# Hybrid decoder trunk: products with v of two pairs of heads in one run

## The chip, the cores and the metric

The kernel runs on one core of a Trainium2 chip. The time is device microseconds of that core, as the median of several executions; one further execution is taken with the hardware profiler, and all durations below come from it. The engines are named as in the profile: PE is TensorE's matmuls, PEld its weight loads, DVE VectorE, ACT ScalarE, POOL GpSimd, SP SyncE.

## What is computed

A trunk of two layers over 256 tokens of width 1024. Each layer normalises its input, projects it, and feeds two mixers: a recurrence (RG-LRU, four blocks of 128 channels here) and an attention with 8 query heads of 64 and 2 key/value heads. Each mixer's output is multiplied by a SiLU gate, and both go through one output projection onto the residual. Cut to what matters for the change:

```python
o_c = einsum('bghqk,bgkd->bghqd', p_c, vc)      # compressed blocks
o_s = einsum('bghqk,bgqkd->bghqd', p_s, vg)     # selected blocks
o_w = einsum('bghqk,bgkd->bghqd', p_w, vwb)     # sliding window
y_b = (gb[..., 0:1] * o_c + gb[..., 1:2] * o_s + gb[..., 2:3] * o_w)
y_b = y_b * silu(nsa_gate)
y = concatenate([y_a, y_b], axis=-1)
return x + y @ w_out
```

## The kernel before

**Tiling.** Activations are held with channels on the 128 partitions and the 256 tokens along the free dimension. A weight is split into a high and a low part (`wh`, `wl`), and so are the activations that it multiplies, so that every large product is three matmuls, made by `mm3` (lines 173 to 175). Two heads, one for each key/value head, share the 128 partitions of a tile; such a pair is called i, and there are four.

**Steps.** A layer is a list of 33 steps, each with one chunk of weights that is loaded, split and multiplied. Steps 0 to 11 of the list `plan` are the twelve chunks of `wf` (three kinds: x and g for the recurrence, n for the attention's gate); 12 to 15 are the first four chunks of the output projection (`out_proj`, half 0, on the recurrence's part of y). Four more chunks of `out_proj` follow (half 1, on the attention's part). The dictionary `SL` (line 53) says ahead of which step each piece of the attention and of the recurrence is written in the program: `att_scores`, `att_coef`, `att_turn`, `att_out`, `rg_gates` and so on. The framework that builds the kernel takes this order as a priority. It sets the order on each engine when the kernel is built, by its own reckoning of when inputs and buffers are ready, and puts in all waits; at run time each engine then works strictly in that order.

**The attention's pieces around the change.** For pair i and token half t:

- `att_scores` and `att_coef` (lines 567 to 607) make scores, exponentials and weights. The last ACT instruction is line 605, which scales the probabilities `pr`.
- `att_turn` (line 609) transposes them on TensorE (line 618) into a `pp` bank, and ACT copies them into the tile `pt` of pair i (`copy`, line 83). `pt` has two buffers, so two pairs can be held at a time.
- `att_out(i)` (line 623) multiplies them with v. The result takes 256 columns of the one PSUM bank of tag `m`. Ten matmuls of 64 output columns each are made, in twos that fill the lower and the upper 64 partitions: per branch two of 256 tokens (line 628) and two of 128 (line 631), then two with the compressed branch's probabilities `pct` (line 634). In the profile each of them has two records, since these operands are plain f32.
- DVE then multiplies the bank with the gate `sgn` into a tile of tag `tmp` (line 636), and `y_split` (line 559) makes the high part on ACT (line 560) and the low part on DVE (line 561), in slot 4 + i of `yy`.

The `m` bank has one buffer. It is used before by the compressed branch (`cmp_scores`, `cmp_pt`) and by each `att_out` in turn, so the next user's matmuls wait until the one before has been read. Before the change, `att_out` stands ahead of steps 6, 7, 12 and 15. Tiles of tag `tmp2` (`pair`, line 227; 128 x 2 x 256, three buffers) are used by the gates, by `rg_gates`, by `rg_out` and, near the layer's end, by the squares for the next norm.

`out_proj` of half 1 needs all four slots of the attention's part. Its first chunk takes the slots 0 to 2 for both output halves first, and slot 3 last (lines 710 to 717), because pair 3 comes last, ahead of step 15.

Of the kernel before, what the change touches and what calls it, by code (L numbers as in the profile page):

```python
# [15 lines left out]
ALU = mybir.AluOpType  # L16
AX = mybir.AxisListType

P = 128
D = 1024  # L20
S = 256
# [3 lines left out]
HD = 64  # L25
# [13 lines left out]
for _n, _w in (("g", 8), ("cw", 16), ("cb", 4), ("br", 4), ("bi", 4), ("lam", 4)):  # L39
# [12 lines left out]
K = dict(scale="A", ev1="A", hid="A", pct="A")  # L52
SL = dict(qk=(0, 2), order=("x0", "x1", "x2", "x3", "n0", "n1", "g0", "g1", "g2", "g3", "n2", "n3"),
          cmp=(2, 3, 4), att=(1, 3, 3, 4, 6, 7, 10, 11), turn=(2, 4, 5, 6, 8, 10,
          12, 13), cs=(5, 5), cpt=6, aout=(6, 7, 12, 15), gates=(2, 3, 4, 5), tab=6, sqrt=5,
          scan=8, rout=(9, 11))


# [13 lines left out]
def hybrid_trunk_kernel(ctx: ExitStack, tc: tile.TileContext, vx, wc, wt, wv, wf, wo, w1, w2, pe,  # L72
# [6 lines left out]
    V, A, G, T = nc.vector, nc.scalar, nc.gpsimd, nc.tensor  # L79
# [7 lines left out]
    def act(shape, tag, bufs=1, dt=F32):  # L87
        return ap_.tile(shape, dt, name=tag, tag=tag, bufs=bufs)

    def bank(tag, bufs, shape=(P, 512), dt=F32):  # L90
        return ps.tile(list(shape), dt, name=tag, tag=tag, bufs=bufs)
# [20 lines left out]
    for n in range(8):  # L112
        T.matmul(wb.rearrange("p (a s) -> p a s", a=2), wz[:, :P], wz[:, None].to_broadcast([P, 2, S]),
                 start=n == 0, stop=n == 7)
# [57 lines left out]
    def mm3(o, lh, ll, rh, rl, start, stop):  # L172
        T.matmul(o, lh, rh, start=start, stop=False)  # L173
        T.matmul(o, lh, rl, start=False, stop=False)  # L174
        T.matmul(o, ll, rh, start=False, stop=stop)  # L175
# [35 lines left out]
    def h_tiles():  # L211
        return act([P, KT, S], "hh", 1, F32R), act([P, KT, S], "hl", 1, F32R)

    def h_split(l, h, k):
        A.activation(h[0][:, k], x_sb[:, k], AF.Copy, scale=v(l, "g", k))
        V.scalar_tensor_tensor(h[1][:, k], x_sb[:, k], v(l, "g", k), h[0][:, k].bitcast(F32),
                               op0=ALU.mult, op1=ALU.subtract)
# [9 lines left out]
    def pair(dt=F32):  # L227
        return act([P, 2, S], "tmp2", 3, dt)
# [27 lines left out]
    def layer(l, prev):  # L256

        L = Layer()
# [300 lines left out]
        def y_split(k, yt):  # L559
            A.copy(L.yy[:, 0, k], yt)  # L560
            V.tensor_tensor(L.yy[:, 1, k], yt, L.yy[:, 0, k].bitcast(F32), op=ALU.subtract)
# [58 lines left out]
                copy(K["ev1"] if c else "A", L.pts[i][:, :, :, t + c],  # L620
                     pp.rearrange("p (g b s) -> p g b s", g=2, b=2))

        def att_out(i):
            pt = L.pts.pop(i)
            yb = L.yb = bank("m", 1)
            for b in range(2):
                for g in range(2):
                    T.matmul(yb[g * HD:(g + 1) * HD, :S], L.vv[:, 0, b, g * HD:(g + 1) * HD],  # L628
                             pt[:, g, b, 0:2].rearrange("p a s -> p (a s)"), start=(b == 0), stop=False)
                for g in range(2):  # L630
                    T.matmul(yb[g * HD:(g + 1) * HD, P:S], L.vv[:, 1, b, g * HD:(g + 1) * HD],
                             pt[:, g, b, 2], start=False, stop=False)
            for g in range(2):
                T.matmul(yb[g * HD:(g + 1) * HD, :S], L.vcb[:, 2 * i + g], L.pct, start=False, stop=True)
            yt = act([P, S], "tmp", 3)
            V.tensor_tensor(yt, yb[:, :S], L.sgn[:, i], op=ALU.mult)
            y_split(4 + i, yt)


        def rg_x(j):  # L640
# [53 lines left out]
        def out_proj(c, half, n):  # L694
            if half and n == 0 and l + 1 < DEPTH:
                L.nh, L.nsq = h_tiles(), act([P, S], "pct")
            last = half and l + 1 == DEPTH and n == 3
            os_ = bank(*OB[half][n])
            os_ = (os_, bank(*FM)) if last else (os_, os_)

            def region(e):
                return os_[e][:, :S] if last else os_[e][:, e * S:(e + 1) * S]

            def products(e, ks):
                for k in ks:
                    mm3(region(e), c.hi[:, k, e * P:(e + 1) * P], c.lo[:, k, e * P:(e + 1) * P],
                        L.yy[:, 0, 4 * half + k], L.yy[:, 1, 4 * half + k],
                        k == 0 and (last or e == 0), k == 3 and (last or e == 1))

            if half and n == 0:  # L710
                products(0, range(3))
                products(1, range(3))
                ks = [3]
            else:
                ks = range(4)
            for e in range(2):
                products(e, ks)
                m = slice(2 * n, 2 * n + 2)
                if last:
                    m = slice(2 * n + e, 2 * n + e + 1)  # L720
                    V.tensor_tensor(x_sb[:, m], x_sb[:, m], region(e)[:, None], op=ALU.add)
                elif e:
                    V.tensor_tensor(x_sb[:, m], x_sb[:, m], os_[0].rearrange("p (a s) -> p a s", a=2), op=ALU.add)  # L723
                else:
                    continue
                if half and l + 1 == DEPTH:
                    nc.sync.dma_start(out[:, m], x_sb[:, m])
                elif half:
                    sk = pair()
                    A.activation(sk, x_sb[:, m], AF.Square)  # L730
                    for k in (2 * n, 2 * n + 1):
                        h_split(l + 1, L.nh, k)
                    if n == 0:
                        L.sk0 = sk
                    else:
                        V.tensor_tensor(L.sk0, L.sk0, sk, op=ALU.add)
                    if n == 3:
                        V.tensor_tensor(L.nsq, L.sk0[:, 0], L.sk0[:, 1], op=ALU.add)
# [8 lines left out]
        for k in range(KT):  # L747
            b = []
# [22 lines left out]
        def at(n, f, *a, mid=False):  # L771
            plan[n][1 if mid else 0].append(F(f, *a))
# [6 lines left out]
        for q in range(8):  # L779
            i, t = divmod(q, 2)  # L780
# [5 lines left out]
        for q in range(8):  # L786
            at(SL["turn"][q], att_turn, *divmod(q, 2))
        for i in range(4):
            at(SL["aout"][i], att_out, i)
            at(SL["gates"][i], rg_gates, i)  # L790
        at(SL["tab"], next_gains, mid=True)
        at(SL["sqrt"], rg_sqrt, mid=True)
# [10 lines left out]
        for half in range(2):  # L803
            for n in range(4):
                step(Chunk(wo[l, 4 * half + n], 4, 256, dma=True),
                     R(out_proj, half, n), None, *(plan[12 + n] if half == 0 else ([], [next_tables] if n == 1 else [])))
# [3 lines left out]
    for l in range(DEPTH):  # L810
        prev, st_ = layer(l, prev)
        prev0 = prev0 or prev
        steps += st_
# [140 lines left out]
```

## Time and profile before

| | |
|---|---|
| median of 3 runs | 253.13 us (252.58 to 253.38) |
| time of the profiled execution | 252.82 us |
| span in that execution, first to last instruction | 251.0 us |
| PE, share of the span with a matmul in flight | 97% |
| DVE, ACT, POOL | 78%, 66%, 16% |
| matmuls of `att_out`, lines 628, 631, 634: records | 64, 64, 32 |
| their mean durations | 392, 273, 379 ns |
| granted TensorE clock | full through the whole span |

The page gives busy time by engine, then groups of instructions by line and shape. A matmul's duration there includes the time in which it shares the array with its neighbours: two that follow one another start 0.12 us apart although each is shown with 0.28. So for TensorE the starts in the time-ordered view are what counts, and the durations of lines tell little. A name such as `m<-pt,vv` gives the tile that is written and those that are read; `128*64` is the weight tile's shape, `128x256` the moving operand's. A bracket behind a row gives the idle time of the engine ahead of it and the instruction that ended it.

### The profile page before, as it was taken

Reading aid. Unit: us, or ns where it says so; the run is one execution under the profiler, and the core shown is the slowest. Engines: PE = TensorE matmul, PEld = TensorE weight load, DVE = VectorE, ACT = ScalarE, POOL = GpSimd, SP = SyncE. Lnnn points to the kernel's source line nnn. Section 1 sums busy time; section 2 is a strip of 40 time slices with the busy share of each in tenths; the row PEclk is TensorE's granted clock in tenths of the full one; section 3 lists DMA queues with packets and bytes.
Section 4 is the critical chain, followed back from the end, with each engine's and each line's share of the span. In section 5 each row is a group of like instructions: output and inputs, shape, how many; then the busy total and the mean of one; then the engine's idle time right before and its main releaser. Section 6 shows DMA issues by size and latency. Waiting matters only on the chain.

```text
span 251.0 us, 5217 instructions
## 1 busy us (share of the span) xinstructions
PE 243.0 (97%) x1958; PEld 222.2 (88%) x1958; DVE 195.8 (78%) x386; ACT 164.5 (66%) x419; POOL 40.1 (16%) x65
## 2 busy tenths in 40 slices
PE   7999998999999999999999999998999999999994
PEld 3989997977899798999999999996889879989993
DVE  4898798879999997654995569688999998765422
ACT  5966419799999967622873553849999996670000
POOL 0034460001811011000001044100100001010000
PEclk9999999999999999999999999999999999999999
DMA  6987999856699688562569878475249858833022
GB/s 211 371 289 226 318 413 407 265 168 202 195 322 403 184 266 293 174 202 72 167 207 347 312 236 263 159 230 187 93 167 347 317 177 268 271 127 84 3 84 84
DMA packets 17593, 57.17 MB, mean 228 GB/s; under 512 B 2208, under 2 KB 3360, under 8 KB 17056
## 3 DMA queue, kind: packets, MB, share of 16 engines
q1 hardware_dynamic: 12816, 39.86, 46.4%
q0 software_dynamic: 4608, 16.78, 20.9%
q8 instruction: 15, 0.25, 0.4%
q10 hardware_dynamic: 144, 0.20, 0.2%
q14 instruction: 10, 0.08, 0.1%
HBM read 55.78 MB, written 1.05 MB: 226 GB/s over the span
## 4 chain that ended last, share of the span: by engine, by line
PE 59%; DVE 19%; ACT 12%; DMA 4%; issue 2%; POOL 1%; SPq 0%; DVEq 0%; ACTq 0%
PE fm L173 11%; PE fm L175 10%; PE fm L174 10%; DVE wl L168 6%; PE s L174 4%; PE s L175 4%; PE s L173 4%; ACT pr L592 3%; PE m L628 3%; PE pp L618 3%; DMA raw<-in_wt_dram 2%; DMA raw<-in_wf_dram 2%; DVE cx L649 2%; POOL st L179 1%; DVE sm L584 1%
## 5 line engine op out<-in xcount | busy, mean ns | idle before, releaser
L168 DVE TENSOR_TENSOR wl<-raw,wh 128x1024 fp32r<-128x1024 f32 (+4 forms) x67 | 74.4, 1117 | 7.9 <-PE pp L174 3.0
L173 PE MATMUL fm<-hh,wh 128*128 128x256 f32 x192 | 56.9, 296 | 0.2
L174 PE MATMUL fm<-hl,wh 128*128 128x256 f32 x192 | 55.0, 287 | 0.0
L175 PE MATMUL fm<-hh,wl 128*128 128x256 f32 x192 | 54.5, 284 | 0.5 <-DVE wl L168 0.5
L165 ACT CAST wh<-raw 128x768 fp32r<-128x768 f32 (+4 forms) x35 | 30.8, 883 | 28.6 <-DMA raw<-in_wc_dram 7.6
L173 PEld LDWEIGHTS fm<-hh,wh 128*128 128x128 f32 x192 | 36.7, 191 | 2.1 <-issue 1.2
L175 PEld LDWEIGHTS fm<-hh,wl 128*128 128x128 f32 x192 | 36.7, 191 | 1.2 <-DVE wl L168 0.8
L174 PEld LDWEIGHTS fm<-hl,wh 128*128 128x128 f32 x192 | 36.7, 191 | 0.5 <-issue 0.4
L592 ACT ACTIVATE pr<-s,sm 128x128 f32<-128x128 f32 (+1 forms) x64 | 26.0, 417 | 9.4 <-DVE sm L586 6.0
L173 PE MATMUL fm<-yy,wh 128*128 128x256 f32 x96 | 27.4, 285 | 0.0
L175 PE MATMUL fm<-yy,wl 128*128 128x256 f32 x96 | 26.8, 279 | 0.0
L174 PE MATMUL fm<-yy,wh 128*128 128x256 f32 x96 | 26.8, 279 | 0.0
L605 ACT ACTIVATE pr<-pr,sm 128x128 f32<-128x128 f32 (+1 forms) x64 | 23.7, 455 | 1.8 <-DVE sm L598 1.8
L173 PEld LDWEIGHTS fm<-yy,wh 128*128 128x128 f32 x96 | 18.0, 188 | 1.5 <-DVE sm L597 0.8
L156 POOL DMA_DIRECT2D wh<-in_wo_dram x16 | 8.5, 530 | 66.2 <-PE fm L175 29.1
L174 PEld LDWEIGHTS fm<-yy,wh 128*128 128x128 f32 x96 | 18.1, 188 | 0.0
L175 PEld LDWEIGHTS fm<-yy,wl 128*128 128x128 f32 x96 | 18.0, 188 | 0.0
L174 PE MATMUL s<-wl,hh 128*128 128x384 f32 x48 | 16.5, 344 | 0.3 <-DVE wl L168 0.3
L723 DVE TENSOR_TENSOR head<-head,fm 128x512 f32<-128x512 f32 x11 | 7.5, 686 | 11.5 <-PE fm L175 11.5
L156 POOL DMA_DIRECT2D wh<-in_wf_dram x16 | 9.0, 565 | 46.2 <-PE fm L175 24.4
L175 PE MATMUL s<-wh,hl 128*128 128x384 f32 x48 | 16.2, 337 | 0.0
L173 PE MATMUL s<-wh,hh 128*128 128x384 f32 x48 | 15.6, 353 | 0.3 <-ACT wh L165 0.3
(205 smaller groups left out, 615.0 us busy)
## 6 DMA issues: line engine op xcount, KB each, us to landing
raw<-in_wf_dram SPq DMA_DIRECT2D x24, 512.0 KB, 4.5
wh<-in_wf_dram POOLq DMA_DIRECT2D x16, 512.0 KB, 4.8
raw<-in_wo_dram SPq DMA_DIRECT2D x16, 512.0 KB, 5.0
wh<-in_wo_dram POOLq DMA_DIRECT2D x16, 512.0 KB, 4.5
raw<-in_wt_dram SPq DMA_DIRECT2D x15, 384.0 KB, 3.9
yy<-in_w_dram SPq DMA_DIRECT2D x4, 1024.0 KB, 7.4
raw<-in_wc_dram SPq DMA_DIRECT2D x4, 512.0 KB, 5.2
raw<-in_wv_dram SPq DMA_DIRECT2D x4, 420.0 KB, 4.9
```

The source lines that it names most:

```text
L156: G.dma_start(self.wh, self.src)
L165: A.copy(hi[:, c], self.raw[:, c])
L168: V.tensor_tensor(lo[:, c], self.raw[:, c], hi[:, c].bitcast(F32), op=ALU.subtract)
L173: T.matmul(o, lh, rh, start=start, stop=False)
L174: T.matmul(o, lh, rl, start=False, stop=False)
L175: T.matmul(o, ll, rh, start=False, stop=stop)
L592: A.activation(pr[g][:, b], ov[:, b], AF.Exp, bias=sm[:, 0, 2 * g + b:2 * g + b + 1], accum_out=sm[:, 1, 2 * g + b:2 * g + b + 1])
L605: A.activation(pr[g][:, b], pr[g][:, b], AF.Copy, scale=sc_)
L618: T.transpose(pp[:, (2 * g + b) * P:(2 * g + b + 1) * P], pr[g][:, b, c * P:(c + 1) * P], ident)
L628: T.matmul(yb[g * HD:(g + 1) * HD, :S], L.vv[:, 0, b, g * HD:(g + 1) * HD], pt[:, g, b, 0:2].rearrange("p a s -> p (a s)"), start=(b == 0) ...
L649: V.scalar_tensor_tensor(cx[:, j], xp[:, 1 + k:1 + k + S], v(l, "cw", 4 * k + j), cx[:, j], op0=ALU.mult, op1=ALU.add)
L723: V.tensor_tensor(x_sb[:, m], x_sb[:, m], os_[0].rearrange("p (a s) -> p a s", a=2), op=ALU.add)
```

## The change

`att_out` now handles two pairs of heads, u = 0 for pairs 0 and 1, u = 1 for pairs 2 and 3. Their products go to the two halves of one `m` bank in one run of twenty matmuls; only the first matmul of the bank for each 64 partitions has the start flag. Then there is one gate product over 512 columns into a `tmp2` tile, and one `y_split` over two slots. The two calls stand ahead of steps 7 and 15. The first chunk of `out_proj`'s half 1 takes the slots 0 and 1 first and then 2 and 3.

```diff
-          12, 13), cs=(5, 5), cpt=6, aout=(6, 7, 12, 15), gates=(2, 3, 4, 5), tab=6, sqrt=5,
+          12, 13), cs=(5, 5), cpt=6, aout=(7, 15), gates=(2, 3, 4, 5), tab=6, sqrt=5,
...
-        def att_out(i):
-            pt = L.pts.pop(i)
-            yb = L.yb = bank("m", 1)
-            for b in range(2):
+        def att_out(u):
+            yb = bank("m", 1)
+            for h in range(2):
+                i = 2 * u + h
+                pt = L.pts.pop(i)
+                o = yb[:, h * S:(h + 1) * S]
+                for b in range(2):
+                    for g in range(2):
+                        T.matmul(o[g * HD:(g + 1) * HD], L.vv[:, 0, b, g * HD:(g + 1) * HD],
+                                 pt[:, g, b, 0:2].rearrange("p a s -> p (a s)"), start=h == b == 0, stop=False)
+                    for g in range(2):
+                        T.matmul(o[g * HD:(g + 1) * HD, P:], L.vv[:, 1, b, g * HD:(g + 1) * HD],
+                                 pt[:, g, b, 2], start=False, stop=False)
                 for g in range(2):
-                    T.matmul(yb[g * HD:(g + 1) * HD, :S], L.vv[:, 0, b, g * HD:(g + 1) * HD],
-                             pt[:, g, b, 0:2].rearrange("p a s -> p (a s)"), start=(b == 0), stop=False)
-                for g in range(2):
-                    T.matmul(yb[g * HD:(g + 1) * HD, P:S], L.vv[:, 1, b, g * HD:(g + 1) * HD],
-                             pt[:, g, b, 2], start=False, stop=False)
-            for g in range(2):
-                T.matmul(yb[g * HD:(g + 1) * HD, :S], L.vcb[:, 2 * i + g], L.pct, start=False, stop=True)
-            yt = act([P, S], "tmp", 3)
-            V.tensor_tensor(yt, yb[:, :S], L.sgn[:, i], op=ALU.mult)
-            y_split(4 + i, yt)
+                    T.matmul(o[g * HD:(g + 1) * HD], L.vcb[:, 2 * i + g], L.pct, start=False, stop=h == 1)
+            yt = pair()
+            V.tensor_tensor(yt, yb.rearrange("p (a s) -> p a s", a=2), L.sgn[:, 2 * u:2 * u + 2], op=ALU.mult)
+            y_split(slice(4 + 2 * u, 6 + 2 * u), yt)
...
             if half and n == 0:
-                products(0, range(3))
-                products(1, range(3))
-                ks = [3]
+                products(0, range(2))
+                products(1, range(2))
+                ks = [2, 3]
...
         for i in range(4):
-            at(SL["aout"][i], att_out, i)
+            if i < 2:
+                at(SL["aout"][i], att_out, i)
             at(SL["gates"][i], rg_gates, i)
```

## The prediction

> **What bounds the kernel now.** I read the page's first two lines, then a table of busy time by stretch, then the instructions in order of time around the code that changes. In the page, busy time and its share of the span:
>
> ```profile
> span 251.0 us, 5217 instructions
> PE 243.0 (97%) x1958; PEld 222.2 (88%) x1958; DVE 195.8 (78%) x386; ACT 164.5 (66%) x419; POOL 40.1 (16%) x65
> ```
>
> In the table by stretch (length, then busy time of each engine, granted clock, DMA share, GB/s), the stretches that hold the changed code:
>
> ```profile
> 80.00:86.00 6.00, 6.00 (x58) 4.38 (x58) 6.00 (x9) 5.97 (x18) 0.53 (x1) 1.00 0.85 285
> 99.00:116.00 17.00, 17.00 (x153) 15.35 (x152) 9.74 (x15) 7.78 (x19) 1.06 (x2) 1.00 0.59 191
> 200.00:205.00 5.00, 4.88 (x50) 3.16 (x48) 4.97 (x9) 4.97 (x14) 0.53 (x1) 1.00 0.56 170
> 205.00:248.00 43.00, 42.43 (x362) 39.94 (x360) 25.34 (x42) 15.50 (x46) 2.65 (x5) 1.00 0.44 140
> ```
>
> TensorE (PE) has work in every one of them, at full clock; DVE and ACT are full only around the first two products of a layer. So what changes TensorE's own time there changes the end by as much. But "busy" only says that some matmul is in flight. What a matmul costs is the distance from one start to the next. The first run of att_out, in order of time (start, duration, line, tile, count):
>
> ```profile
> 80.53 0.28 PE L175 MATMUL fm<-hh,wl 128*128 128x256 f32 x1
> 80.65 0.28 PE L173 MATMUL fm<-hh,wh 128*128 128x256 f32 x1
> 80.86 0.44 PE L628 MATMUL m<-pt,vv 128*64 128x256 f32 x2
> ...
> 81.12 0.39 PE L628 MATMUL m<-pt,vv 128*64 128x256 f32 x2
> 81.34 0.39 PE L631 MATMUL m<-pt,vv 128*64 128x128 f32 x4
> 81.56 0.39 PE L628 MATMUL m<-pt,vv 128*64 128x256 f32 x2
> ...
> 81.78 0.39 PE L628 MATMUL m<-pt,vv 128*64 128x256 f32 x2
> ...
> 82.21 0.39 PE L634 MATMUL m<-pct,vcb 128*64 128x256 f32 x2
> ...
> 82.42 0.39 PE L634 MATMUL m<-pct,vcb 128*64 128x256 f32 x2
> 82.74 0.66 PE L618 MATMUL pp<-cst,pr 128*128 128x128 f32 x4
> 83.15 0.36 PE L174 MATMUL fm<-hl,wh 128*128 128x256 f32 x1
> ```
>
> And the second run's end:
>
> ```profile
> 85.15 0.60 PE L634 MATMUL m<-pct,vcb 128*64 128x256 f32 x4
> 85.68 0.38 PE L175 MATMUL fm<-hh,wl 128*128 128x256 f32 x1
> 85.90 0.28 PE L173 MATMUL fm<-hh,wh 128*128 128x256 f32 x1
> ```
>
> Two fm matmuls stand 0.12 us apart (80.53, 80.65). From the last fm to the run's first matmul it is 0.21: **0.09 lost on entering**. The matmuls of a run write 64 columns each and go in pairs. Inside the run a pair of 256 takes 0.22 (81.12 to 81.34, 81.56 to 81.78), but the first took 0.26: **0.04 more**. The last pair (82.42) is followed after 0.32 instead of 0.22: **0.10 on leaving**; and the first full-width matmul after a run holds the next back by 0.22 instead of 0.12 (85.68 to 85.90): **0.10 more**. A run thus costs 0.33 us beyond its matmuls. There are 8 runs, all of ten matmuls (20 records).
>
> **The change, part by part.**
>
> *Fewer runs.* Four runs of one pair of heads in each layer become two of two pairs, with the same matmuls. Four entries and four leavings go. Three of them save 0.33. The run at 80.86 is left into transposes (82.74): four of those and the next start take 0.41 where eight take 0.79 (104.80 to 105.59, below), about 0.05 too much, so there it is 0.09 + 0.04 + 0.10 + 0.05 = 0.28. Sum: 3 x 0.33 + 0.28 = **1.27 us**. No row shows the seam between two pairs of heads inside one run. Its cost lies between 0 (the run's inner steps, as from 81.56 to 81.78, change line and weights freely) and the whole 0.33; I take 0, since at the seam the 64-column shape stays, as in those rows.
>
> The Trainium skill, "TensorEngine Tiling (Array Packing)", section "Tiling Modes / Key Properties", states that a change of tiling mode drains TensorE, while a change of tile alone does not. It gives no time. The Trainium skill, "TensorE: Matmul & The Clock Gate", Part 2 ("Step-by-step"), puts a drain at about 128 cycles, 53 ns at 2.4 GHz. An estimate from the two pages: four runs have eight changes of mode, 8 x 0.053 = 0.43 us, against 1.27 by the rows. The rows decide: entering and leaving cost more here than such a drain.
>
> *A wait that goes.* All att_out results use the one "m" bank, so a run must wait until DVE has read the one before. In the second layer that is visible:
>
> ```profile
> 202.39 0.60 PE L618 MATMUL pp<-cst,pr 128*128 128x128 f32 x4
> 202.66 0.40 DVE L636 TENSOR_TENSOR tmp<-m,sgn 128x256 f32<-128x256 f32 x1
> 203.11 0.20 PEld L628 LDWEIGHTS m<-pt,vv 128*64 128x64 f32 x4 [0.36 <-DVE tmp L636]
> ...
> 99.47 0.60 PE L618 MATMUL pp<-cst,pr 128*128 128x128 f32 x4
> 100.00 0.65 PE L628 MATMUL m<-pt,vv 128*64 128x256 f32 x4
> ```
>
> From four transposes to a run takes 0.72 there and 0.53 elsewhere: **0.19 us** goes, as both pairs now sit in one bank. Next late at this place would be the transposed probabilities of the second pair; ACT's copies are started at 199.96 and take 1.08 together, done at 201.04, and the second half would begin at 200.17 + 1.73 = 201.9 (a run takes 80.86 to 82.74, 1.88, less 0.14 of entering and leaving inside it). So nothing.
>
> ```profile
> 199.96 1.08 ACT L83 COPY pt<-pp 128x512 f32<-128x512 f32 x2
> ```
>
> *Gate product and split.* Per two pairs: two products L636 and two splits L561 of 256 columns, 0.42 us each, become one each of 512; two ACT copies L560 become one. Rows for the wide forms exist, from rg_out:
>
> ```profile
> 87.85 0.69 DVE L682 TENSOR_TENSOR tmp<-tl,sgr 128x512 f32<-128x512 f32 x1
> 89.59 0.60 ACT L560 CAST yy<-tmp 128x512 fp32r<-128x512 f32 x1
> 90.23 0.69 DVE L561 TENSOR_TENSOR yy<-tmp,yy 128x512 fp32r<-128x512 f32 x1 [0.22 <-ACT yy L560]
> ```
>
> DVE saves 2 x (0.84 - 0.69) = 0.30 and ACT about 0.2 per run. Neither is what TensorE waits for in these stretches, so I count 0. The result tile moves from the "tmp" ring to the "tmp2" ring of three, which also holds gate tiles and rg_out's. No row shows that ring full; if it were, the product would queue for one more wide instruction, 0.7 us, and DVE's later work behind it. Between 0 and 0.7 per run, on an engine that TensorE isn't waiting for: 0. At the seam DVE now reads the first pair only when the second is done, 1.73 us later; nothing needs that result before out_proj's second half.
>
> *The second run's place.* Products of the third pair of heads move from step 12 to step 15, so their split is done later. out_proj covers it with 12 instead of 18 matmuls, besides the 24 of the chunk before:
>
> ```profile
> 233.28 0.42 DVE L636 TENSOR_TENSOR tmp<-m,sgn 128x256 f32<-128x256 f32 x1
> 233.74 0.41 ACT L560 CAST yy<-tmp 128x256 fp32r<-128x256 f32 x1 [7.32 <-DVE tmp L636]
> 234.18 0.42 DVE L561 TENSOR_TENSOR yy<-tmp,yy 128x256 fp32r<-128x256 f32 x1 [0.47 <-ACT yy L560]
> ...
> 236.07 0.28 PE L173 MATMUL s<-yy,wh 128*128 128x256 f32 x1
> ```
>
> The chain takes 1.3 us now and about 0.69 + 0.60 + 0.69 + 0.1 = 2.1 then; the cover from the run's end is 36 x 0.12 = 4.3 us. An L168 and an L723 ahead of it on DVE (1.2 + 0.7) still fit. Cost 0, 0.3 if all of it came together with more.
>
> Moving 1.73 us of matmuls (and 0.33 of switching) away from step 12 also takes cover from somebody: everything on TensorE between steps 12 and 15 comes 2.06 us earlier, while ACT does not. First in line are the transposes of the last probabilities (att_turn(3,1), L618):
>
> ```profile
> 102.33 1.71 ACT L605 ACTIVATE pr<-pr,sm 128x256 f32<-128x256 f32 x4 [0.71 <-DVE sm L598]
> ...
> 104.80 1.03 PE L618 MATMUL pp<-cst,pr 128*128 128x128 f32 x8
> 105.59 0.36 PE L173 MATMUL fm<-yy,wh 128*128 128x256 f32 x1
> ...
> 222.24 1.71 ACT L605 ACTIVATE pr<-pr,sm 128x256 f32<-128x256 f32 x4 [0.70 <-DVE sm L598]
> ...
> 224.71 1.03 PE L618 MATMUL pp<-cst,pr 128*128 128x128 f32 x8
> ```
>
> ACT is done at 104.04; TensorE came at 104.80 and would come at 102.74. The fourth transpose, 0.33 later, would wait **1.0 us**; in the second layer (223.95 against 224.71) the same. But TensorE's order isn't the program's: the framework that builds the kernel places an instruction where it reckons its inputs ready. Where transposes came early in the first layer, it put single fm matmuls between them, and TensorE lost nothing:
>
> ```profile
> 64.00 0.37 PE L173 MATMUL fm<-hh,wh 128*128 128x256 f32 x1
> 64.20 0.38 PE L618 MATMUL pp<-cst,pr 128*128 128x128 f32 x2
> ```
>
> It may put matmuls of the next out_proj chunk ahead here in the same way. So this costs 0 to 2.0 in all; I take 0, by the rows at 64, and name it as the first rival.
>
> **Sum** against the profiled execution: 252.82 (span 251.0 and 1.8 around it) - 1.27 - 0.19 = 251.4. The median of the runs shown, 253.13, lies 0.3 above that execution: **251.6 us**.
>
> **Rivals.**
> 1. *The transposes of the last pair wait for ACT.* The gain of 1.46 is given back at L618 in both layers, 1.0 each: 253.13 - 1.46 + 2.0 = 253.7, slower than before. It decides from 0.73 per layer. For it: the 0.76 us of slack quoted above against 2.06 of shift. Against it: the order is made anew. Chance 0.25, partial waits (252.3 to 253.3) included.
> 2. *The run doesn't stay in one piece, or the seam costs like a switch.* Then fm matmuls stand between the pairs, or the seam loses what entering and leaving lose, and 1.27 shrinks to between 8 x 0.04 (the first pair's excess, taken as all that a change of shape costs) and 0.7: 252.2 to 252.6. This is also where the Trainium skill's drain ("TensorEngine Tiling (Array Packing)", as above) would put it. For it: in the first layer fm matmuls were put between the runs. Against it: between those runs the bank had to be read, which falls away. Chance 0.13.
> 3. *The new order brings a new stall elsewhere.* TensorE idles 251.0 - 243.0 = 8.0 us now; a third of that anew, 2.7, where DVE and ACT are full (80 to 86), gives 253.13 - 1.46 + 2.7 = 254.4. For it: everything after the first run is placed anew. Against it: DVE and ACT have less to do. Chance 0.07.
> 4. *DVE's savings reach TensorE too*, half of 4 x 0.30: 251.0. Chance 0.05; TensorE's gap-free stretches speak against it.
>
> The forecast itself has 0.5, with 251.1 to 252.2 around it.
>
> **How the numbers follow.** About 0.3% (0.76 us) is what a measurement of this kernel can tell from no change. Faster by more, below 252.37: 0.50 + 0.05 + 0.07 from rivals 1 and 2 = 0.62. Slower, above 253.89: 0.07 + 0.02 from rival 1 = 0.09. Between: 0.29. The range runs from 251.0 (forecast less the 0.5 by which runs differ) to 253.4, which takes in rival 2 and most of rival 1.
>
> **What would show it.** Two runs per layer of 40 records each, with no other matmul between, the first pair 0.26 and later ones 0.22, at the seam too. No wait for the gate product before a run. At L618 (3,1): a start within 0.12 us of the matmul before says no wait; idle time "<-ACT pr L605" says rival 1. DVE 0.69 at the product. TensorE's gap-free stretches stay gap-free. The prediction is wrong if runs are broken up, if L618 waits over 0.7 us per layer, or if idle TensorE time appears that isn't in the rows above.

## The result

| | before | after |
|---|---|---|
| median of 5 runs | 252.84 us (252.22 to 253.38) | 251.25 us (250.81 to 252.19) |
| ratio after / before, 95% interval | | 0.9945 [0.9925, 0.9964] |
| profiled execution: time, span | 252.82, 251.0 us | 251.37, 249.6 us |

The changed kernel's median is 1.6 us lower. The ratio, whose interval leaves out 1, puts the gain at 0.55%. Its page begins:

```profile
span 249.6 us, 5207 instructions
PE 241.3 (97%) x1958; PEld 222.6 (89%) x1958; DVE 195.3 (78%) x378; ACT 164.5 (66%) x415; POOL 39.8 (16%) x65
```

The matmuls are as many as before (1958 records). DVE has eight instructions less and ACT four. TensorE is busy for 1.7 us less, though it does the same products. The first run of the changed kernel, in order of time (line 632 was 628, 638 was 634):

```profile
79.95 0.28 PE L175 MATMUL fm<-hh,wl 128*128 128x256 f32 x1
80.08 0.28 PE L173 MATMUL fm<-hh,wh 128*128 128x256 f32 x1
80.28 0.44 PE L632 MATMUL m<-pt,vv 128*64 128x256 f32 x2
...
81.64 0.60 PE L638 MATMUL m<-pct,vcb 128*64 128x256 f32 x4
82.07 0.39 PE L632 MATMUL m<-pt,vv 128*64 128x256 f32 x2
...
83.37 0.60 PE L638 MATMUL m<-pct,vcb 128*64 128x256 f32 x4
83.90 0.66 PE L618 MATMUL pp<-cst,pr 128*128 128x128 f32 x4
84.31 0.36 PE L174 MATMUL fm<-hl,wh 128*128 128x256 f32 x1
```

Forty records stand in one piece. At the seam two pairs of line 638 take 0.43 us (81.64 to 82.07), the 0.22 each of any pair inside a run: the seam costs nothing. At the end the same two pairs take 0.53 (83.37 to 83.90), so leaving still costs 0.10.

**Where the time went.** Two starts on TensorE are easily found again in every version: the compressed branch's transposes (line 536), before the first run of a layer, and the first product of `out_proj`'s second half, after the last run, which goes to a bank named `s`. Between them lies all that the change touches. The rows of the kernel before (its last mark, 236.07, stands in the prediction), and after:

```profile
77.45 0.38 PE L536 MATMUL m<-cst,sc 128*128 128x128 f32 x2
116.16 0.28 PE L173 MATMUL s<-yy,wh 128*128 128x256 f32 x1
198.64 0.41 PE L536 MATMUL m<-cst,sc 128*128 128x128 f32 x2
```

```profile
76.87 0.38 PE L536 MATMUL m<-cst,sc 128*128 128x128 f32 x2
115.27 0.28 PE L173 MATMUL s<-yy,wh 128*128 128x256 f32 x1
198.07 0.41 PE L536 MATMUL m<-cst,sc 128*128 128x128 f32 x2 [0.25 <-DVE sm L598]
234.62 0.28 PE L173 MATMUL s<-yy,wh 128*128 128x256 f32 x1
```

The same four marks, taken from the trace of every kernel that was run, give this table (differences of the unrounded starts). The first column holds no changed instruction. The third holds only the changed order of slots in the first chunk of half 1, with the same matmuls.

| us | start to mark 1 | layer 1 stretch | between | layer 2 stretch |
|---|---|---|---|---|
| before | 77.45 | 38.71 | 82.48 | 37.43 |
| after | 76.87 | 38.39 | 82.80 | 36.55 |
| after, once more | 77.59 | 38.39 | 82.49 | 36.55 |
| four runs, wide product | 77.26 | 38.71 | 82.65 | 37.22 |
| two runs, narrow products | 77.31 | 38.41 | 82.45 | 36.54 |
| second run in 4 parts | 77.38 | 39.44 | 82.40 | 37.58 |
| second run in 10 parts | 76.88 | 41.58 | 82.52 | 39.72 |
| last transposes later | 77.06 | 38.03 | 82.59 | 36.54 |
| the same, once more | 77.50 | 38.02 | 82.52 | 36.55 |

These two columns scatter by up to 0.7 and 0.4 us; the stretches, where they hold the same runs and transposes, by 0.02. So the change is worth **0.32 us in the first layer and 0.88 in the second, 1.20 in all**; the 1.4 us between the two spans are that, plus 0.58 at the start, less 0.32 between. What scatters between the stretches is a load that DVE waits for; its row before, and after:

```profile
191.90 1.23 DVE L168 TENSOR_TENSOR wl<-raw,wh 128x1024 fp32r<-128x1024 f32 x1 [0.48 <-DMA raw<-in_wf_dram]
```

```profile
191.33 1.22 DVE L168 TENSOR_TENSOR wl<-raw,wh 128x1024 fp32r<-128x1024 f32 x1 [0.80 <-DMA raw<-in_wf_dram]
```

In all nine traces the third column is 82.0 us plus this idle time, to 0.04 us in eight of them and to 0.1 in the ninth.

### The profile page after: what moved, and what is told of

Its sections match the earlier page's. It is cut to its first block, busy times and chain, and to the rows that moved or that the text cites. A ratio compares the mean times of both kernels' runs of the same rounds, so it can differ in the third digit from the quotient of the medians.

```text
span 249.6 us, 5207 instructions
## 1 busy us (share of the span) xinstructions
PE 241.3 (97%) x1958; PEld 222.6 (89%) x1958; DVE 195.3 (78%) x378; ACT 164.5 (66%) x415; POOL 39.8 (16%) x65
## 4 chain that ended last, share of the span: by engine, by line
PE 66%; DVE 13%; ACT 12%; DMA 6%; issue 2%; SPq 0%; DVEq 0%; ACTq 0%
PE fm L173 11%; PE fm L175 11%; PE fm L174 11%; DVE wl L168 5%; PE s L174 4%; PE s L175 4%; PE s L173 4%; PE pp L618 3%; PE m L632 3%; ACT pr L592 3%; DMA head<-in_vx_dram 3%; DMA raw<-in_wf_dram 2%; DVE cx L653 2%; PE pp L175 2%; PE pp L174 2%
```

## The experiments

The theory is that of the prediction: the gain is TensorE's entering and leaving of the 64-column shape, and a wait on one bank. The first rival to it is the other half of the change, the gate product and split over 512 columns.

**Four runs, but one bank and one wide product.** Against the kernel before:

```diff
-          12, 13), cs=(5, 5), cpt=6, aout=(6, 7, 12, 15), gates=(2, 3, 4, 5), tab=6, sqrt=5,
+          12, 13), cs=(5, 5), cpt=6, aout=(6, 9, 12, 15), gates=(2, 3, 4, 5), tab=6, sqrt=5,
...
-            yb = L.yb = bank("m", 1)
+            if i % 2 == 0:
+                L.yb = bank("m", 1)
+            yb = L.yb[:, i % 2 * S:i % 2 * S + S]
...
-            yt = act([P, S], "tmp", 3)
-            V.tensor_tensor(yt, yb[:, :S], L.sgn[:, i], op=ALU.mult)
-            y_split(4 + i, yt)
+            if i % 2:
+                yt = pair()
+                V.tensor_tensor(yt, L.yb.rearrange("p (a s) -> p a s", a=2), L.sgn[:, i - 1:i + 1], op=ALU.mult)
+                y_split(slice(3 + i, 5 + i), yt)
```

The first chunk of half 1 takes its slots in the order of the change here too.

> Four runs per layer as before (the second pair's ahead of step 9, so that it can't join the first), but the two halves of one bank, one gate product and one split over 512 columns. Theory (the gain is TensorE's entries to and leavings from the 64-column shape): only the 0.19 us wait on the bank goes, 252.65 us, ratio to before 0.999. Rival (the wide gate product and split make the gain): 251.25 us, ratio 0.9945.

Measured: 252.1 us against 252.49 of before, ratio 0.9985 [0.9972, 0.9999]. The first layer's stretch is as before to the hundredth (38.71), the second's 0.21 shorter: the wait on the bank, put at 0.19. The second run also stands 2.65 us later here (205.76 instead of 203.11), away from the product that it waited for, so this run doesn't tell the shared bank from the later place. The wide product, the wide split and the order of slots by themselves bring nothing.

**Two runs, narrow products.** Against the changed kernel:

```diff
-            yt = pair()
-            V.tensor_tensor(yt, yb.rearrange("p (a s) -> p a s", a=2), L.sgn[:, 2 * u:2 * u + 2], op=ALU.mult)
-            y_split(slice(4 + 2 * u, 6 + 2 * u), yt)
+            for i in (2 * u, 2 * u + 1):
+                yt = act([P, S], "tmp", 3)
+                V.tensor_tensor(yt, yb[:, i % 2 * S:i % 2 * S + S], L.sgn[:, i], op=ALU.mult)
+                y_split(4 + i, yt)
```

> Two runs per layer as in the change, but four gate products and four splits of 256 columns, as before. Theory: the gain stays, 251.25 us, ratio 0.9945 (within 0.2%), and in the trace every run has its first pair 0.26 and all later pairs 0.22 us apart. Rival (wide product and split): back to 252.8 us, ratio 1.0.

Measured: 251.34 us against 252.49, ratio 0.9956 [0.9942, 0.997]; stretches 38.41 and 36.54, those of the change. In its trace the first two pairs of a run take 0.48 us together and two later ones 0.43, as expected. With the run before, this settles it: the runs make the gain, and the width of the DVE and ACT work makes none.

**The price of one more run.** In the changed kernel, the second run of each layer was cut and its parts were put between the matmuls of the `out_proj` chunk that follows it, in program order; `between` stands after each of `mm3`'s three matmuls and issues the next part, after the last one also the gate product and the split.

```diff
+CUTS = [(0, 1), (1, 2), (2, 3), (3, 4), (4, 5), (5, 6), (6, 7), (7, 8), (8, 9), (9, 10)]
...
+    def between(now):
+        if hooks and now:
+            hooks.pop(0)()
+            if len(hooks) == 1:
+                hooks.pop(0)()
...
         T.matmul(o, lh, rh, start=start, stop=False)
+        between(True)
```

> The change, but in each layer the second run is cut into its ten pairs of matmuls with one full-width matmul of the output projection between two of them: nine more entries and leavings per layer, 18 in all, with the same matmuls. Theory: 0.33 us each as read from the profile of before, so 251.25 + 5.9 = 257.2 us, ratio to before 1.017. If only the first pair's 0.04 us is the price of a change of shape: 252.0 us, ratio 0.997. If a change of shape costs nothing and the gain came from elsewhere: 251.25 us, ratio 0.9945.

Measured: 257.57 us against 252.49, ratio 1.0202 [1.0183, 1.0221]. The order of time shows what each part costs:

```profile
109.66 0.44 PE L645 MATMUL m<-pt,vv 128*64 128x128 f32 x4
110.03 0.38 PE L184 MATMUL fm<-yy,wh 128*128 128x256 f32 x1
110.34 0.65 PE L641 MATMUL m<-pt,vv 128*64 128x256 f32 x4
110.93 0.39 PE L186 MATMUL fm<-yy,wl 128*128 128x256 f32 x1
```

Two pairs of 128 and one full-width matmul take 0.68 us (109.66 to 110.34). Undisturbed they take 0.22 + 0.12. So one entering and leaving costs 0.34. From the stretches: (41.58 - 38.39) / 9 = 0.354, and (39.72 - 36.55) / 9 = 0.352 in the second layer.

The Trainium skill, "TensorEngine Tiling (Array Packing)", section "Tiling Modes / Key Properties", has a change of tiling mode drain TensorE and a change of tile not. The trace agrees on both: no cost at the seam, where the upper and lower 64 columns alternate, and 0.35 us for one entering and leaving. The estimate from the drain that the Trainium skill, "TensorE: Matmul & The Clock Gate", Part 2 ("Step-by-step"), puts at about 128 cycles, two times 0.053 us, is a third of that.

The same with four parts (`CUTS = [(0, 2), (2, 5), (5, 7), (7, 10)]`), and three full-width matmuls between two of them (`between` acts only after the third matmul of `mm3`):

> The change, but in each layer the second run is cut into four parts with one product of the output projection (three full-width matmuls) between two of them: three more entries and leavings per layer, six in all. The run cut into ten parts cost 0.353 us for each. Theory (a price per change of shape, whatever stands between): 251.25 + 6 x 0.35 = 253.35 us, ratio to before about 1.003, and both stretches with a second run 1.05 us longer in the trace. Rival (the ten parts were dear because single matmuls left no time to fetch weights ahead): less than half of that, 252.3 us or less, ratio 0.998.

Measured: 253.23 us against 252.21, ratio 1.0031 [1.0014, 1.0047]; stretches 39.44 and 37.58, which is (39.44 - 38.39) / 3 = 0.35 and (37.58 - 36.55) / 3 = 0.34 for each part. One full-width matmul between or three, the price is the same: it hangs on the change of shape, not on how many matmuls stand between to cover the next weight load.

**Shape or operand type.** The narrow matmuls differ from their neighbours in a second way: their operands are plain f32 (two records each), while those of `mm3` are float32r (`fp32r` in the rows that write them; one record each). The trace of the kernel before tells the two apart. `rg_gates` (line 657) has plain f32 matmuls at full width, and behind two of them stand two full-width transposes into the same `m` bank (line 515):

```profile
189.60 0.28 PE L175 MATMUL fm<-hh,wl 128*128 128x256 f32 x1
189.72 1.02 PE L657 MATMUL fm<-cx,rws 128*128 128x256 f32 x4
190.58 0.38 PE L515 MATMUL m<-cst,tmp 128*128 128x128 f32 x2
190.71 0.36 PE L173 MATMUL fm<-hh,wh 128*128 128x256 f32 x1
190.92 0.28 PE L174 MATMUL fm<-hl,wh 128*128 128x256 f32 x1
```

The four records of line 657 take 0.86 us, 0.215 each, the pace inside a run, where two narrow matmuls share the array and four records take 0.43. From 189.60 to 190.92 it is 1.32 us: 0.86, two transposes with 0.22 (as from 77.45 to the next start at 77.67) and two matmuls of `mm3` with 0.12 each. So a change of type and of bank at full width costs nothing here to 0.01 us, and the 0.34 belongs to the shape.

A part of the price can be seen in the weight loads. In the kernel before, at the end of a run:

```profile
204.99 0.19 PEld L173 LDWEIGHTS fm<-hh,wh 128*128 128x128 f32 x1 [0.39 <-issue]
204.99 0.38 PE L173 MATMUL fm<-hh,wh 128*128 128x256 f32 x1
...
205.10 0.19 PEld L174 LDWEIGHTS fm<-hl,wh 128*128 128x128 f32 x1
...
205.22 0.28 PE L174 MATMUL fm<-hl,wh 128*128 128x256 f32 x1
```

Between matmuls of one shape the load starts 0.12 us ahead of its matmul (205.10 for 205.22); behind the change of shape it starts with it (204.99 for both), and so it does on entering (80.86 for both). Whether the late load is the whole price, no run here shows.

**What the first layer lost.** Two runs fewer at 0.34 should have shortened the first layer's stretch by 0.6 to 0.7 us, but it got 0.32. The changed kernel, TensorE and then ACT, where the last pair's probabilities are transposed:

```profile
101.57 0.28 PE L174 MATMUL fm<-yy,wh 128*128 128x256 f32 x1
101.68 0.28 PE L175 MATMUL fm<-yy,wl 128*128 128x256 f32 x1
101.98 0.44 PE L618 MATMUL pp<-cst,pr 128*128 128x128 f32 x2
102.17 0.36 PE L173 MATMUL fm<-yy,wh 128*128 128x256 f32 x1
102.38 0.44 PE L618 MATMUL pp<-cst,pr 128*128 128x128 f32 x2
102.58 0.36 PE L174 MATMUL fm<-yy,wh 128*128 128x256 f32 x1
102.78 0.44 PE L618 MATMUL pp<-cst,pr 128*128 128x128 f32 x2
102.97 0.36 PE L175 MATMUL fm<-yy,wl 128*128 128x256 f32 x1
103.18 0.28 PE L173 MATMUL fm<-yy,wh 128*128 128x256 f32 x1
103.30 0.38 PE L618 MATMUL pp<-cst,pr 128*128 128x128 f32 x2
```

```profile
101.42 1.71 ACT L605 ACTIVATE pr<-pr,sm 128x256 f32<-128x256 f32 x4 [0.70 <-DVE sm L598]
```

The framework put single matmuls of `out_proj` between the transposes, as the prediction had hoped, but each two transposes still come up against the ACT instruction that scales their input: they start 0.40 us apart (101.98, 102.38, 102.78), near ACT's pace (1.71 for four), where two transposes and a matmul take 0.34 without a wait, and the first starts 0.30 after the matmul before it instead of 0.12. The 0.18 there and three times 0.06 behind it make 0.36. In the second layer ACT is done at 220.44 and TensorE comes at 221.53, with nothing to wait for:

```profile
218.73 1.71 ACT L605 ACTIVATE pr<-pr,sm 128x256 f32<-128x256 f32 x4 [0.50 <-DVE sm L598]
...
221.53 1.03 PE L618 MATMUL pp<-cst,pr 128*128 128x128 f32 x8
```

There the new order has ACT scale them earlier against TensorE than before. The test is to put these transposes one step later:

```diff
-          12, 13), cs=(5, 5), cpt=6, aout=(7, 15), gates=(2, 3, 4, 5), tab=6, sqrt=5,
+          12, 14), cs=(5, 5), cpt=6, aout=(7, 15), gates=(2, 3, 4, 5), tab=6, sqrt=5,
```

> The change, but the last transposes (pair 3, second token half) one step later, ahead of step 14. In the changed kernel's first layer they stand in twos between single matmuls of the output projection, and TensorE loses about 0.38 us there, waiting for ACT line 605. Theory: that loss goes, 250.9 us, ratio to before 0.993. Rival: the later copies of the transposed tile hold up the second run, or the first layer's gain is taken back by the second layer's wait on a load: 251.25 us or more, ratio 0.9945 or above.

Measured: 250.86 us against 252.49, ratio 0.9939 [0.9925, 0.9952]. All eight transposes stand together again:

```profile
104.68 0.28 PE L175 MATMUL fm<-yy,wl 128*128 128x256 f32 x1
104.80 1.03 PE L618 MATMUL pp<-cst,pr 128*128 128x128 f32 x8
105.59 0.37 PE L173 MATMUL fm<-yy,wh 128*128 128x256 f32 x1
```

The first layer's stretch is 38.03, 0.68 below before and 0.36 below the change; the second layer's stays at 36.54. The changed kernel and this version once more, side by side:

> The changed kernel once more, beside the version with the later transposes on the same chip. Theory: ratio to before 0.9945 to 0.9955. In the trace the stretch of the second layer in which no instruction differs from before (from the second layer's first gate chunk to the transposes of the compressed branch) takes 40.8 to 41.0 us if the 41.14 of the first profile is a scatter of load times, and 41.1 again if the change brings it.

> The version with the transposes of the last pair ahead of step 14, once more beside the changed kernel. Theory: 0.3 to 0.4 us faster than the changed kernel, ratio to before 0.993 to 0.994; in the trace the first layer's stretch with the two runs takes 38.03 us against 38.40. Rival: no difference to the changed kernel beyond its scatter.

Measured against 252.21 of before: the change 251.71 us, ratio 0.997 [0.9953, 0.9987]; later transposes 250.96 us, ratio 0.9941 [0.9923, 0.9958]. The medians put 0.75 us between the two versions, more than the 0.3 to 0.4 expected; the first layer's stretch puts 0.37 (38.39 and 38.02). The stretches repeat to 0.01 us. The one between the layers' stretches is 82.49 for the change this time (its part that was expected at 40.8 to 41.0 takes 40.8, as in the kernel before), so the 82.80 of its first profile was scatter of load times, not the change. The change's ratio misses what was expected, 0.9945 to 0.9955, and is nearer to 1 than in the first comparison (0.9945); the 1.20 us of the stretches, a ratio of 0.9953, lies inside the first interval and on the edge of the second. The version with the later transposes beats both kernels; 0.68 + 0.89 = 1.57 us by its stretches, a ratio of 0.9938, which both its measurements meet.

## Why the prediction was right

- **The bound.** Right. TensorE's starts set the time; what was saved there arrived at the end undiminished (from the last mark to the end of the span it is 15.0 us in the kernels before and after).
- **Fewer runs, 1.27 us.** Right in mechanism and size. A run was put at 0.33 by reading starts; the cut runs give 0.34 to 0.35 for each. The four runs that went brought (by the stretches of the version with the later transposes, less the bank's 0.21) 0.68 + 0.89 - 0.21 = 1.36. One of the four was put at 0.28, as the run that is left into transposes; but the run of two pairs is still left into them (83.90), so what went was another 0.33.
- **The seam at 0.** Right: 0.43 for its two pairs, as inside a run.
- **The wait on the bank, 0.19.** Right in size: 0.21 in the version with four runs, where the bank is shared and the second run also stands later.
- **Gate product and split, 0.** Right: 36.54 and 36.55 with narrow and with wide ones. The 0.30 that DVE saves per run in its own time shows in neither stretch.
- **The later split of the third pair, 0.** Right. The chain after the last run, DVE and then ACT in the changed kernel:

```profile
231.83 0.69 DVE L640 TENSOR_TENSOR tmp<-m,sgn 128x512 f32<-128x512 f32 x1 [1.80 <-PE m L638]
233.21 0.69 DVE L561 TENSOR_TENSOR yy<-tmp,yy 128x512 fp32r<-128x512 f32 x1 [0.69 <-ACT yy L560]
```

```profile
232.55 0.62 ACT L560 CAST yy<-tmp 128x512 fp32r<-128x512 f32 x1 [9.31 <-DVE tmp L640]
```

  It takes 2.07 us (2.1 was put) and ends at 233.90; the second half begins at 234.62 and needs it 12 matmuls later.
- **The transposes of the last pair, 0 of a possible 2.0.** This term was mis-sized, and with it the sum: 1.46 forecast, 1.20 measured in the stretches. The first rival holds in small. The transposes do wait for ACT, in the first layer alone and for 0.36 us instead of 1.0, with matmuls put between them. It was named with its place and reason. The step that failed in the sum is the 0, taken from the rows at 64, where TensorE lost nothing: in the first layer ACT's four instructions came later than the places that the transposes were given, so matmuls put between hid only a part.
- **The time.** 251.6 forecast (253.13 less 1.46 is 251.67), 251.25 measured. That the two are this close owes something to scatter: 1.20 us below 252.84 would be 251.64.

## What to carry to other kernels

Read matmuls by the distance between their starts, not by their durations: the 0.35 us for each excursion into another array shape shows in no busy share and no wait of PE. Its one sign beside the starts is that the first weight load behind a change of shape starts only with its matmul (204.99, where 0.39 us of idle time is put down to `issue`). Put products of a narrow shape into as few runs as buffers allow, and count the runs. When a block of work is moved on the engine that sets the end, look at what it used to cover: here 0.36 of the 0.68 us that the first layer should have gained went to the first instruction behind the old place that waits for another engine, and moving that one step later got it back.

## What was not expected of the hardware

Entering and leaving the narrow shape costs the same 0.34 to 0.35 us whether one or three full-width matmuls stand between two narrow parts, so excursions simply add up: 18 of them made 6.4 us (3.19 + 3.17 by the stretches). And the trace repeats a stretch bounded by TensorE to 0.01 or 0.02 us between executions, while the first 77 us, with the first loads in them, scatter by 0.7; the stretches settle differences that whole-kernel times, with 250.58 to 252.3 for one and the same kernel, leave in doubt.
